# A written order for the expert stage's TensorE, VectorE and ScalarE work, with a split lead of 7 to 3 tiles, 7 of 14 down tiles kept in float32, and three more tile buffers

## The chip, the core and the metric

The kernel runs on one core of one Trainium2 chip. The core has five engines with a queue each: PE (TensorE, whose weight loads the profile shows as PEld), DVE (VectorE), ACT (ScalarE), POOL (GpSimd) and SP (SyncE, which here only issues DMAs). Each engine works its own queue strictly in the order of the program; semaphores tie them together. The metric is the device time in microseconds. The median of three runs of the kernel before is 1290.66 us (1288.96 to 1290.76).

## The reference

Two layers over 256 positions of width 1024. Each layer runs a mixer and a channel mixer. The second layer's channel mixer is the stage that this case is about: eight experts of width 3584, and each position takes its two best.

```python
def swiglu(x, wg, wu, wd):
    return (jax.nn.silu(x @ wg) * (x @ wu)) @ wd

def moe_swiglu(h, w_router, wg, wu, wd):
    xt = h.reshape(-1, d)
    logits = (xt @ w_router).astype(jnp.float32)
    top_v, top_i = lax.top_k(logits, TOP_K)
    gates = jax.nn.softmax(top_v, axis=-1)
    comb = jnp.sum(jax.nn.one_hot(top_i, N_EXPERTS) * gates[..., None], axis=1)
    y = jnp.zeros_like(xt)
    for e in range(N_EXPERTS):
        y = y + comb[:, e:e + 1] * swiglu(xt, wg[e], wu[e], wd[e])
    return y.reshape(bsz, s, d)
```

All weights are float32 in HBM.

## The kernel before

**Tiles.** All large weights come as one stream of 406 tiles of 128 x 2048 float32 (1 MB). Tiles 0 to 69 belong to the first mixer, the dense layer and the second mixer; tiles 70 to 405 are the experts': eight experts times 14 column groups (`NG`) times three tiles (gate, up, down). One group of one expert is called a step here, numbered n = 0 to 111. `MOE` is 70.

**Split.** A product is made of float16 parts. `split_tile` (L101) turns a raw tile into a high part on ACT (L114, called the heads) and a remainder on DVE (L115, the tails; it needs the heads). `mm3` (L276) then does three float16 products: high x high (L278), high x low (L279) and low x high (L280), which is the first to need the tails. Some down tiles are not split but used as they are in float32: `whole(i)` (L119) says so for groups 1, 4, 7 and 10 of the 14 (`WHOLE`), 32 tiles in all.

**A step.** `gate_up` (L414) does the 96 products of the gate and the up tile for the at most 80 positions of the expert (`CAP`); `hidden` (L436) makes silu on ACT (L446), the product on DVE (L450, or L448 where the down tile is whole) and, for a split down tile, its two float16 parts (L452 on ACT, L453 on DVE). `down` (L607) of the step before follows: 12 float16 products (L621) for a split tile, four float32 products (L615) for a whole one. Once per expert come `gather` (L548: 16 float32 products L558, parts L562 on ACT and L563 on DVE, for the next expert's input), `scatter_weights` (L593), `evacuate` (L625) and `combine` (L631: four float32 products L636, sums L637 on DVE).

**Buffers.** Raw tiles sit in `RAW` = 9 slots and, in the experts, in two more "spare" tiles put together from work buffers (`SPARE`, loaded as two halves each), again and again in a ring of 11. Split tiles sit in `SPLIT` = 9 buffers. A raw slot is free again when the tails are made, or, for a whole tile, when its `down` is done. `load` (L84) issues the DMAs on SP in tile order, and a DMA whose slot is still in use holds SP and every DMA behind it.

**Order.** The code calls `split` up to the step after the current one (L646), but the queue order of all engines is set by a scheduler at build time from its own estimates of durations; nothing in the code fixes where the heads of a tile stand against the silu of a step on ACT.

Of the kernel before, what the change touches and what calls it, by code (L numbers as in the profile page):

```python
# [7 lines left out]
F32 = mybir.dt.float32  # L8
F16 = mybir.dt.float16
# [22 lines left out]
RAW = 9  # L32
# [4 lines left out]
SPARE = (("gw", "ig"), ("a", "th"))  # L37

WHOLE = (1, 4, 7, 10)
# [13 lines left out]
def trunk(ctx: ExitStack, tc: tile.TileContext, x, w, small, gates, last, out):  # L53
# [27 lines left out]
    state = {"loaded": 0, "split": 0}  # L81
    NT = w.shape[0]

    def load(upto):  # L84
        while state["loaded"] < min(upto, NT):
# [14 lines left out]

    def split_tile(i, r):  # L101

        t = spl.tile([P, 2, 2048], F16, name="hl")
        fine = isinstance(i, int) and MOE + SPLIT - 1 <= i < MOE + SPLIT + 3
        with ExitStack() as order:
            if i == MOE + SPLIT - 1:
                for ins in behind:
                    order.enter_context(tc.issue_after(ins))
            for sl, src in r:
                n = sl.stop - sl.start  # L110
                step = 512 if fine else n
                for k in range(0, n, step):
                    to = slice(sl.start + k, sl.start + k + step)
                    S.activation(t[:, 0, to], src[:, k:k + step], AF.Copy, scale=SW)  # L114
                    V.scalar_tensor_tensor(t[:, 1, to], src[:, k:k + step], SW, t[:, 0, to], op0=OP.mult,  # L115
                                           op1=OP.subtract)
        parts[i] = [t[:, 0], t[:, 1]]

    def whole(i):  # L119

        return i >= MOE and (i - MOE) % 3 == 2 and (i - MOE) // 3 % NG in WHOLE

    def split(upto):
        while state["split"] < min(upto, NT):
# [7 lines left out]
            load(i + 1 + RAW + (len(SPARE) if i >= MOE else 0))  # L132
# [281 lines left out]
    def gate_up(ig, iu, h, n, between=None):  # L414

        if isinstance(iu, int):
            split(iu + 1)
# [77 lines left out]
    def moe(l, accs, extra_load):  # L495
        base = pos["t"]
        gcol = par["nf"][:, l * 8:(l + 1) * 8]
# [50 lines left out]
        def gather(e):  # L548
            oh = wk.tile([P, 2, CAP], F32, name="oh", tag="rs", bufs=2)
            for c in range(2):  # L550
                V.tensor_scalar(oh[:, c], iota1, slot[:, c, e:e + 1], rS[:, c:c + 1], op0=OP.is_equal, op1=OP.mult)
            he = wk.tile([P, KD, 2, CAP], F16, name="he", tag=("uc", "ge")[e % 2])
            for q in range(4):
# [283 lines left out]
```

## Time and profile before

| | us |
|---|---|
| median of three runs | 1290.66 |
| the profiled execution, its own time | 1290.75 |
| its span, first to last instruction | 1288.9 |
| PE busy | 1193.8 (93%) |
| DVE busy | 1056.8 (82%) |
| ACT busy | 868.0 (67%) |

The span is 1.85 us shorter than the execution's own time. "Busy" is time with an instruction on the engine; PE's matmuls are pipelined, so its share is no measure of how close it is to its peak. The experts take the stretch from about 416 us to the end.

### The profile page before, as it was taken

The numbers are of one execution on the slowest core, as the hardware profiler recorded it, in microseconds if no ns is written. First come the engines' busy times: TensorE is split into PE (matmuls) and PEld (weight loads), VectorE is DVE, ScalarE is ACT, GpSimd is POOL, SyncE is SP. The second block draws the span as 40 slices with busy tenths as digits, with TensorE's granted clock in tenths as the row PEclk, the third lists the DMA queues.
The fourth block names the chain that finished last, engine by engine and source line by source line (L and its number), as shares of the span: only waits on it lengthen the run. The fifth ranks groups of instructions, "written<-read, shape, count | busy, mean of one in ns | idle before, by whom it ended". The sixth has DMA issues, their size and how long they took to land. (4 is left out here: it accounts for less than half of the span.)

```text
span 1288.9 us, 35355 instructions
## 1 busy us (share of the span) xinstructions
PE 1193.8 (93%) x15792; PEld 934.6 (73%) x15792; DVE 1056.8 (82%) x1083; ACT 868.0 (67%) x942; POOL 0.8 (0%) x7
## 2 busy tenths in 40 slices
PE   7999999999999999999899888999898899989986
PEld 5888888888889777776566666666766666666663
DVE  7797655567886998988788989898798898989885
ACT  6965444445674977768567767776677687777774
POOL 0000000000000000000000000000000000000000
PEclk9999999999997999999899999999999999999997
DMA  9975555554554999999999999999999999999970
GB/s 366 372 280 220 204 198 199 205 207 172 199 191 160 363 414 417 407 417 408 394 399 382 416 364 382 419 351 417 417 416 395 416 419 414 418 418 399 417 317 35
DMA packets 69282, 431.87 MB, mean 335 GB/s; under 512 B 7808, under 2 KB 7936, under 8 KB 24960
## 3 DMA queue, kind: packets, MB, share of 16 engines
q1 hardware_dynamic: 69120, 429.52, 83.6%
q8 instruction: 125, 2.05, 0.6%
q14 instruction: 37, 0.30, 0.1%
HBM read 428.44 MB, written 1.05 MB: 333 GB/s over the span
## 5 line engine op out<-in xcount | busy, mean ns | idle before, releaser
L115 DVE SCALAR_TENSOR_TENSOR hl<-raw,hl 128x2048 f16<-128x2048 f32 (+2 forms) x336 | 728.3, 2190 | 141.9 <-ACT hl L114 140.2
L114 ACT ACTIVATE hl<-raw 128x2048 f16<-128x2048 f32 (+2 forms) x336 | 603.2, 1824 | 94.4 <-PE mm L280 87.0
L280 PEld LDWEIGHTS <-hl 128*128 128x128 f16 x4704 | 469.0, 100 | 117.2 <-DVE hl L115 90.7
L278 PEld LDWEIGHTS <-hl 128*128 128x128 f16 x4704 | 470.4, 100 | 53.8 <-issue 18.7
L279 PEld LDWEIGHTS <-hl 128*128 128x128 f16 x4704 | 470.6, 100 | 32.3 <-issue 11.3
L280 PE MATMUL mm<-he,hl 128*128 128x80 f16 x3584 | 410.2, 203 | 59.2 <-DVE hl L115 57.1
L278 PE MATMUL mm<-he,hl 128*128 128x80 f16 x3584 | 416.0, 203 | 7.4 <-ACT hl L114 6.9
L279 PE MATMUL mm<-he,hl 128*128 128x80 f16 x3584 | 415.7, 203 | 0.0
L621 PE MATMUL acc<-hl,hdm 128*80 128x512 f16 x960 | 233.5, 382 | 2.1 <-DVE hdm L453 1.2
L278 PE MATMUL mm<-h,hl 128*128 128x256 f16 x768 | 209.3, 274 | 3.0 <-ACT h L228 2.8
L279 PE MATMUL mm<-h,hl 128*128 128x256 f16 x768 | 209.8, 274 | 1.8 <-DVE h L229 1.6
L280 PE MATMUL mm<-h,hl 128*128 128x256 f16 x768 | 209.9, 274 | 0.8 <-DVE hl L115 0.8
L621 PEld LDWEIGHTS <-hdm 128*80 128x80 f16 x960 | 102.5, 118 | 73.3 <-issue 3.3
L446 ACT ACTIVATE sg<-mm 128x160 f32<-128x160 f32 x112 | 33.7, 301 | 149.5 <-PE mm L280 149.4
L615 PE MATMUL acc<-raw,hdm 128*80 128x512 f32 x216 | 101.5, 599 | 0.0
L279 PE MATMUL acc<-hd,hl 128*128 128x256 f16 x224 | 60.9, 273 | 0.2 <-DVE hd L453 0.2
L280 PE MATMUL acc<-hd,hl 128*128 128x256 f16 x224 | 60.9, 273 | 0.0
L278 PE MATMUL acc<-hd,hl 128*128 128x256 f16 x224 | 60.6, 273 | 0.0
L452 ACT ACTIVATE hdm<-sg 128x160 f16<-128x160 f32 x80 | 26.7, 333 | 48.2 <-DVE sg L450 48.0
L615 PEld LDWEIGHTS acc<-raw,hdm 128*80 128x80 f32 x216 | 29.1, 151 | 34.9 <-issue 34.6
L636 PE MATMUL mm<-ye,sgt 80*128 80x512 f32 x64 | 37.0, 715 | 4.3 <-ACTq L664 3.1
L558 PE MATMUL mm<-oh,xt 128*128 128x80 f32 x256 | 35.6, 295 | 0.5 <-DVE sg L450 0.5
(207 smaller groups left out, 854.0 us busy)
## 6 DMA issues: line engine op xcount, KB each, us to landing
raw<-in_w SPq DMA_DIRECT2D x345, 1024.0 KB, 12.2
gw<-in_w SPq DMA_DIRECT2D x29, 512.0 KB, 11.8
ig<-in_w SPq DMA_DIRECT2D x29, 512.0 KB, 12.1
a<-in_w SPq DMA_DIRECT2D x29, 512.0 KB, 11.5
th<-in_w SPq DMA_DIRECT2D x29, 512.0 KB, 12.0
raw<-in_w SPq DMA_DIRECT2D x6, 512.0 KB, 11.9
xT<-in_x SPq DMA_DIRECT2D x4, 256.0 KB, 3.7
gw<-in_gates SPq DMA_DIRECT2D x2, 512.0 KB, 9.9
```

The lines of the kernel that those rows point to most:

```text
L114: S.activation(t[:, 0, to], src[:, k:k + step], AF.Copy, scale=SW)
L115: V.scalar_tensor_tensor(t[:, 1, to], src[:, k:k + step], SW, t[:, 0, to], op0=OP.mult, op1=OP.subtract)
L278: PE.matmul(o, wt[0][:, cols], a_hi, start=start, stop=False, skip_group_check=True)
L279: PE.matmul(o, wt[0][:, cols], a_lo, start=False, stop=False, skip_group_check=True)
L280: PE.matmul(o, wt[1][:, cols], a_hi, start=False, stop=stop, skip_group_check=True)
L446: S.activation(sg, bank[:, 0], AF.Silu, scale=scale)
L452: S.activation(hd[:, 0, sl], hf, AF.Copy)
L558: PE.matmul(o[:, z], xt[:, c, k * P:(k + 1) * P], oh[:, c], start=(z == 0 and c == 0), stop=(c == 1), skip_group_check=True)
L615: PE.matmul(eaccs[e][q], hd[:, c], wt[c][:, q * half:(q + 1) * half], start=(g == 0 and c == 0), stop=(g == NG - 1 and c == 1), skip_group ...
L621: PE.matmul(eaccs[e][q], hd[:, part, c], wt[wpart][:, c * D + q * half:c * D + (q + 1) * half], start=(g == 0 and c == 0 and part == 0 and ...
L636: PE.matmul(o, sgt[e][:, c * P:(c + 1) * P], ye[:, sl], start=True, stop=True)
```

## The change

Before the experts the engines' order stays as it was. `RAW` goes from 9 to 11, and there are three spares, (gw, ig), (a, th) and (cs, r), each used once, for tiles 90, 91 and 92. The room for the two more slots comes from a smaller DMA scratch (`dynamic_dma_scratch_size=1024`). `whole` takes every sixth tile, the down tile of each odd step: 56 tiles, seven of 14 per expert. In the experts the queues of PE, DVE and ACT follow the program text (`tc.manual_schedule`), while SP's is still set by the scheduler. A step is written as: `gate_up`, half a `combine` or a quarter of a `gather` where one is due, the `down` of the step before; on ACT and DVE beside it the heads and tails of two or three tiles, with silu behind the first heads. Splits run `LEAD` tiles ahead of the step's up tile, 7 falling to 3 over the 112 steps (as whole numbers: 7 in the first step, then 6, 5, 4 and 3 for about a quarter each), and heads one tile further.

```diff
-RAW = 9
+RAW = 11
-SPARE = (("gw", "ig"), ("a", "th"))
-WHOLE = (1, 4, 7, 10)
+SPARE = (("gw", "ig"), ("a", "th"), ("cs", "r"))
+LEAD = (7.0, 3.0)
+FIRST_SPARE = MOE + 9 + RAW
     def load(upto):
-            at = (i - MOE - SPLIT - RAW) % (RAW + len(SPARE))
-            if i >= MOE + SPLIT + RAW and at < len(SPARE):
+            at = i - FIRST_SPARE
+            if 0 <= at < len(SPARE):
     def whole(i):
-        return i >= MOE and (i - MOE) % 3 == 2 and (i - MOE) // 3 % NG in WHOLE
+        return i >= MOE and (i - MOE) % 6 == 5
+        def next_heads():
+            ...
+            heads(*halves[i])
+        def next_tails():
+            ...
+            todo["n"] += 1
+            tails(*halves.pop(i))
+            load(i + 1 + RAW + len(SPARE))
+            for n, (e, g) in enumerate(steps):
+                bank = gate_up(ig, iu, lambda part, k: he[:, k, part], CAP)[0]
+                if ready is not None and n > 1:
+                    combine(*ready, c=(g - 1))
+                ...
+                if 8 <= g < 12 and e + 1 < NE:
+                    gather_products(e + 1, g - 8)
+                if n:
+                    down(*before)
+                used = 2 * (n + 1) + (n + 1) // 2
+                lead = LEAD[0] + (LEAD[1] - LEAD[0]) * n / (len(steps) - 1)
+                k = max(0, used + int(lead) - todo["n"])
+                ...
+                if n == 0:
+                    next_heads()
+                for j in range(k + 2):
+                    if j < k:
+                        next_heads()
+                    if j == 0:
+                        S.activation(sg, bank[:, 0], AF.Silu, scale=IN_SCALE)
+                    if j < k:
+                        next_tails()
+                    if j == 0:
+                        V.scalar_tensor_tensor(hd if whole(idn) else hf, bank[:, 1], ...)
+                    if j == 1 and not whole(idn):
+                        S.activation(hd[:, 0], hf, AF.Copy)
+                        V.tensor_tensor(hd[:, 1], hf, hd[:, 0], op=OP.subtract)
+                ...
+        with tc.manual_schedule(engines={mybir.EngineType.PE, mybir.EngineType.DVE, mybir.EngineType.Activation}):
+            before = groups()
```

ACT's queue at steps 46 to 48 (the fourth expert), before: sg is the silu of a step, hl the heads of a tile, hdm the high part of the step's result.

```order
L446 ACTIVATE sg_10982<-mm 128x160
L114 ACTIVATE hl<-raw 128x2048 x4
L446 ACTIVATE sg_11111<-mm 128x160
L114 ACTIVATE hl<-raw 128x2048
L452 ACTIVATE hdm<-sg_11112 128x160
L114 ACTIVATE hl<-raw 128x2048 x2
L446 ACTIVATE sg_11234<-mm 128x160
L114 ACTIVATE hl<-raw 128x2048
L452 ACTIVATE hdm<-sg_11235 128x160
L114 ACTIVATE hl<-gw 128x1024
L114 ACTIVATE hl<-ig 128x1024
```

The same steps on ACT in the changed kernel (sgt is a copy that falls into step 46 once per expert):

```order
L737 ACTIVATE sg_10790<-mm 128x160
L113 ACTIVATE hl<-raw 128x2048
L745 ACTIVATE hdm<-sg_10791 128x160
L754 ACTIVATE sgt<-mm 80x256
L113 ACTIVATE hl<-raw 128x2048
L737 ACTIVATE sg_10920<-mm 128x160
L113 ACTIVATE hl<-raw 128x2048 x3
L737 ACTIVATE sg_11041<-mm 128x160
L113 ACTIVATE hl<-raw 128x2048
L745 ACTIVATE hdm<-sg_11042 128x160
L113 ACTIVATE hl<-raw 128x2048
```

The kinds of work stay the same; what moves is which tiles' heads these are (further ahead of the step), and the regular two or three per step.

PE's queue around the gather of the second expert's input, in the first expert's step 11, before:

```order
L280 MATMUL mm<-he,hl 128x80
L558 MATMUL mm<-oh,xt 128x80 x16
L615 MATMUL acc<-raw,hdm 80x512 x4
L278 LDWEIGHTS hl
L278 MATMUL mm<-he,hl 128x80
```

In the changed kernel, the second of four such places (step 9 of the first expert):

```order
L289 MATMUL mm<-he,hl 128x80
L574 MATMUL mm<-oh,xt 128x80 x4
L639 MATMUL acc<-raw,hdm 80x512 x4
L287 LDWEIGHTS hl
L287 MATMUL mm<-he,hl 128x80
```

The 16 products in one block have become four products in each of the steps 8 to 11, between `gate_up` and `down`.

SP's queue from the last load ahead of the experts on, before (cs<-in_last is a constant for the end of the kernel; TENSOR_LOAD reads the longest list):

```order
L94 DMA raw<-in_w 128x2048
L727 DMA cs<-in_last 128x1024
L94 DMA raw<-in_w 128x2048 x5
L650 TENSOR_LOAD mxi
L650 ISA x2
L94 DMA raw<-in_w 128x2048 x6
L94 DMA gw<-in_w 128x1024
L94 DMA ig<-in_w 128x1024
L94 DMA a<-in_w 128x1024
L94 DMA th<-in_w 128x1024
L94 DMA raw<-in_w 128x2048 x9
```

In the changed kernel:

```order
L97 DMA raw<-in_w 128x2048
L97 DMA cs<-in_w 128x1024
L97 DMA raw<-in_w 128x2048 x2
L760 TENSOR_LOAD mxi
L760 ISA x2
L97 DMA raw<-in_w 128x2048 x10
L834 DMA cs<-in_last 128x1024
L97 DMA raw<-in_w 128x2048 x301
L97 DMA raw<-in_w 128x1024 x4
```

The spares no longer return; the constant now stands behind twelve expert loads, where it waits until tile 92, which sits in cs, is split.

## Rows read from the trace of the kernel before

**Rows 1.** The page: span, and busy time of each engine.

```profile
span 1288.9 us, 35355 instructions
PE 1193.8 (93%) x15792; PEld 934.6 (73%) x15792; DVE 1056.8 (82%) x1083; ACT 868.0 (67%) x942; POOL 0.8 (0%) x7
```

**Rows 2.** Stretches: from:to, length, busy by engine, granted clock, DMA share, GB/s.

```profile
480.00:1200.00 720.00, 657.76 (x10195) 481.28 (x10192) 626.17 (x558) 517.50 (x527) 0.00 (x0) 0.99 1.00 404
1200.00:1250.00 50.00, 46.26 (x711) 32.87 (x708) 42.74 (x33) 37.82 (x33) 0.00 (x0) 0.97 0.99 406
1250.00:1252.00 2.00, 2.00 (x39) 1.40 (x38) 2.00 (x2) 0.00 (x0) 0.00 (x0) 1.00 0.13 53
1000.00:1150.00 150.00, 137.31 (x2151) 100.78 (x2152) 131.12 (x117) 109.91 (x115) 0.00 (x0) 1.00 1.02 416
500.00:550.00 50.00, 50.00 (x785) 36.60 (x784) 44.29 (x41) 36.29 (x38) 0.00 (x0) 1.00 1.01 410
800.00:850.00 50.00, 45.15 (x676) 33.46 (x674) 42.96 (x44) 35.69 (x42) 0.00 (x0) 0.97 1.02 419
```

**Rows 3.** Waits from 416 to 1271 us: who waited for whom, us, times, longest.

```profile
PEld L280 <- DVE hl L115: 89.5, 96, 2.7
PEld L278 <- ACT hl L114: 11.7, 16, 3.2
ACT sg L446 <- PE mm L280: 149.4, 91, 6.9
DVE hl L115 <- ACT hl L114: 68.3, 61, 3.3
DVE hl L115 <- DMA th<-in_w: 1.5, 1, 1.5
SPq L94 <- PE acc L615: 109.7, 27, 11.3
```

**Rows 4.** Timeline of ACT: the silus of steps that PE runs without a wait.

```profile
540.14 0.30 ACT L446 ACTIVATE sg<-mm 128x160 f32<-128x160 f32 x1 [1.04 <-PE mm L280]
...
546.12 0.30 ACT L446 ACTIVATE sg<-mm 128x160 f32<-128x160 f32 x1 [1.12 <-PE mm L280]
...
553.09 0.30 ACT L446 ACTIVATE sg<-mm 128x160 f32<-128x160 f32 x1 [1.80 <-PE mm L280]
```

**Rows 5.** Groups by form, 460 to 1240 us: count, busy us, mean ns, idle before.

```profile
L115 DVE SCALAR_TENSOR_TENSOR hl<-raw,hl 128x2048 f16<-128x2048 f32 x221 | 499.0, 2284 | 64.8 <-ACT hl L114 63.3 <-DMA th<-in_w 1.5
L114 ACT ACTIVATE hl<-raw 128x2048 f16<-128x2048 f32 x219 | 408.9, 1900 | 0.8 <-PE mm L280 0.8
L115 DVE SCALAR_TENSOR_TENSOR hl<-ig,hl 128x1024 f16<-128x1024 f32 x27 | 32.8, 1214 | 0.0
L446 ACT ACTIVATE sg<-mm 128x160 f32<-128x160 f32 x101 | 30.5, 302 | 142.6 <-PE mm L280 142.4
L453 DVE TENSOR_TENSOR hdm<-sg,hdm 128x160 f16<-128x160 f32 x72 | 22.8, 317 | 3.0 <-ACT hdm L452 3.0
L637 DVE TENSOR_TENSOR xT<-mm,xT 128x512 f32<-128x512 f32 x24 | 15.8, 684 | 5.6 <-PE mm L636 5.4
L563 DVE SCALAR_TENSOR_TENSOR he<-mm,sm,he 128x80 f16<-128x80 f32 x56 | 14.7, 293 | 9.4 <-ACT he L562 9.4
```

**Rows 6.** Timeline of PE near 700 us: gather, whole down, split down.

```profile
701.70 2.09 PEld L558 LDWEIGHTS mm<-oh,xt 128*128 128x128 f32 x18
...
703.78 3.60 PE L615 MATMUL acc<-raw,hdm 128*80 128x512 f32 x8
...
708.06 1.46 PE L621 MATMUL acc<-hl,hdm 128*80 128x512 f16 x6
```

**Rows 7.** The entry: SP's issues from 397 to 446 us.

```profile
397.55 0.33 SPq L727 DMA_DIRECT2D cs<-in_last  x1
416.57 29.61 SPq L94 DMA_DIRECT2D raw<-in_w  x11
```

**Rows 8.** Timeline: ACT's first silu, PE's last down; then the chain's combine.

```profile
419.57 1.28 ACT L446 ACT_TABLE_LOAD   x1
420.87 0.30 ACT L446 ACTIVATE sg<-mm 128x160 f32<-128x160 f32 x1
...
1268.22 2.32 PE L621 MATMUL acc<-hl,hdm 128*80 128x512 f16 x10
...
1273.64 7.21 PE mm L636 x8
```

**Rows 9.** Stretches of 5 us with a low DMA rate or a low clock.

```profile
765.00:770.00 5.00, 5.00 (x73) 3.22 (x72) 5.00 (x3) 4.31 (x3) 0.00 (x0) 1.00 0.69 257
855.00:860.00 5.00, 5.00 (x72) 3.22 (x68) 4.98 (x4) 2.26 (x3) 0.00 (x0) 1.00 0.43 152
830.00:835.00 5.00, 5.00 (x67) 3.72 (x65) 5.00 (x4) 3.01 (x4) 0.00 (x0) 0.70 1.03 420
```

More of the change, by code (lines that the diff above doesn't have):

```diff
@@ L496, in moe @@
         base = pos["t"]
+        state["experts"] = True
+        split(MOE + 8)
+        load(FIRST_SPARE + len(SPARE))
         gcol = par["nf"][:, l * 8:(l + 1) * 8]
@@ L567, in moe, with gather_products @@
-        hes = {0: gather(0)}
-        gathered = hes[0][1]
+                V.tensor_scalar(lists[e][:, c], iota1, slot[:, c, e:e + 1], rS[:, c:c + 1], op0=OP.is_equal,
+                                op1=OP.mult)
+            hes[e] = wk.tile([P, KD, 2, CAP], F16, name="he", tag=("uc", "ge")[e % 2])
+        def gather_products(e, q):
+            o = got[e, q] = mm((P, 2, CAP))
+            for z in range(2):
+                k = 2 * q + z
+                for c in range(2):
+                    PE.matmul(o[:, z], xt[:, c, k * P:(k + 1) * P], lists[e][:, c], start=(z == 0 and c == 0),
+                              stop=(c == 1), skip_group_check=True)
@@ L637, in combine @@
                     V.tensor_tensor(yt[:, c, sl], o, (xt if e == 0 else yt)[:, c, sl], op=OP.add)
-        before, ready = None, None
-        for e, g in steps:
-            ig, iu, idn = take(3)
-            he = hes[e][0]
-            banks = gate_up(ig, iu, lambda part, k: he[:, k, part], CAP)
-            hd = [P, 2, CAP] if whole(idn) else [P, 2, 2, CAP]
-            hd = hidden(banks, CAP, wk.tile(hd, F32 if whole(idn) else F16, name="hdm", tag="xs", bufs=2))
-            split(idn + 1 + 3)
-            if g == 3:
-                scatter_weights(e)
-            if e == 0 and g == 2:
-                longest = nc.values_load(mxi[0:1, 0:1], min_val=0, max_val=T)
-            if e == NE - 1 and g == 0:
-                extra_load()
-            if g == 11 and e + 1 < NE:
-                hes[e + 1] = gather(e + 1)
-            if ready is not None:
-                combine(*ready)
-                ready = None
-            if before is not None:
-                down(*before)
-                if before[1] == NG - 1:
-                    ready = (before[0], evacuate(before[0]))
-            before = (e, g, idn, hd)
+        for i in (MOE + 8, MOE + 9):
+            t = spl.tile([P, 2, 2048], F16, name="hl")
+            with ExitStack() as order:
+                if i == MOE + 8:
+                    for ins in behind:
+                        order.enter_context(tc.issue_after(ins))
+                for hi, lo, src in split_pieces(raw.pop(i), t, 512):
+                    S.activation(hi, src, AF.Copy, scale=SW)
+                    V.scalar_tensor_tensor(lo, src, SW, hi, op0=OP.mult, op1=OP.subtract)
+            parts[i] = [t[:, 0], t[:, 1]]
@@ new lines, in moe @@
+        todo = {"heads": MOE + 10, "tails": MOE + 10, "n": 9}
+        halves = {}
+        def next_heads():
+            while todo["heads"] < NT and whole(todo["heads"]):
+                i = todo["heads"]
+                parts[i] = [t[:, k:k + D] for _, t in raw.pop(i) for k in range(0, t.shape[1], D)]
+                todo["heads"] += 1
+            i = todo["heads"]
+            if i == NT:
+                return
+            todo["heads"] += 1
+            t = spl.tile([P, 2, 2048], F16, name="hl")
+            halves[i] = (raw.pop(i), t)
+            heads(*halves[i])
+            parts[i] = [t[:, 0], t[:, 1]]
```

130 lines of the change are left out of this document (86 added, 44 removed).

## The prediction

> **What bounds the kernel now.** I read the page first: PE is busy for 93% of the span and DVE for 82% [rows 1], which says that several engines are near their limit and not which of them ends last. So I went to the experts' stage, from 416 us on, and read three things there. The stretches: from 480 to 1200 us the DMA moves 404 GB/s, but over 1000 to 1150 us it holds 416 [rows 2]. So DMA runs at 97% of a rate that it can hold, and 3% is lost in places; two of them are in [rows 9] (257 and 152 GB/s over 5 us). The waits: PE waits 89.5 us in 96 pieces for the tails of a split and 11.7 us for heads [rows 3], 101 us in all, 0.9 us a step. ACT waits 149.4 us for `gate_up` at the silu, and DVE 68.3 us for heads, but only one wait, of 1.5 us, is for a landing [rows 3]. So the tiles are there and the splits come late. The reader should see a loop in this: the silu stands in ACT's queue and waits for PE; heads behind it, of tiles that have long landed, wait too; DVE's tails wait for the heads; and PE, one step on, waits for the tails. The timeline of ACT shows the same steps without that wait: 5.98 us from silu to silu with a split down and 6.97 us with a whole one [rows 4].
>
> So two limits stand close together: the loop sets the pace, and the DMA is 3% behind it. The last load lands at about 1251 us, when 53 GB/s are left over 2 us [rows 2]; the last `down` ends at 1268.22 + 2.32 = 1270.5 us [rows 8], and 18.4 us of combine, norm and output follow to the end of the span [rows 1, 8]. All the tiles that were landed or split by 1251 us still had to go through PE.
>
> **The change, part by part.**
>
> *Written order, lead 7 to 3.* It takes the heads that PE needs next out from behind the silu that PE must release: a tile is split three to six tiles ahead of the step that uses it. What PE must do with no wait, per expert: seven steps of 5.98 and seven of 6.97 us [rows 4] are 90.7 us; the gather has 32 pieces at 2.09 / 18 = 0.116 us, 3.7 us [rows 6]; the combine took 7.21 us at the end at half the clock, so 3.6 us at full clock [rows 8]. That is 98.0 us, or 7.0 us a step. DVE, per expert: 35 tails x 2.28 = 79.8; 21 small ones x 0.32 = 6.7; eight of 0.29 and four of 0.68 are 5.1; with lists some 93 us [rows 5]. ACT: 35 x 1.90 = 66.5, and with its small ones some 77 us [rows 5]. DMA: 42 tiles of 1.049 MB at 416 GB/s are 105.9 us [rows 2]. The order of limits is then DMA, PE, DVE, ACT, if no wait is left. In a pair of steps DVE has 5 tails and 3 small ones, 12.4 us, against 12.95 us of PE, so the tails hold a lead where it exists. With the lead at 3, the up tile of the next step is only just ready: silu 0.30, two tails and two small ones, 5.5 us, against a whole down of 3.44 us and half of a `gate_up` (1.7 us), so about 0.4 us lost in every second step of the last quarter, 6 us in all. PE has 0.56 us a step to spare against DMA, which covers it.
>
> *Seven whole down tiles instead of four.* It removes 24 splits (24 x 2.28 = 55 us of DVE, 24 x 1.90 = 46 us of ACT) and adds 24 x 0.99 = 24 us to PE [rows 4, 5]. In a DMA-bound stage none of the three is on the path. Without that cover PE pays the 24 us.
>
> *Buffers.* Before, SP stands idle from 397.55 to 416.57 us for want of a slot [rows 7]. Now three more tiles are loaded in this gap (3.1 MB, 7.6 us at 416 GB/s). Against it: the spares free no slot of the ring when they are split, and the constant for the end holds SP until tile 92 is split, so part of the gain can be given back before 480 us. I bound it by 0 and 7.6 us and take 5.
>
> *Reading the longest list* moves from the end into step 2 on three engines. The rows do not show it in such a place; I take it as nothing, within 1 us either way, since all three engines have slack there.
>
> *DMA's end.* From 480 us on the kernel before moved 720 x 404 + 50 x 406 + 2 x 53 GB/s, that is 311.3 MB [rows 2]. At a steady 416 GB/s this takes 748 us and ends at 1228; less 5 us for the spares, 1223 us.
>
> The Trainium skill's page "DMA: Bandwidth & Descriptors" (Specifications) gives a limit of some 358 GB/s from HBM for one core; at that rate the same bytes would end at about 1341 us and the run at about 1371. The trace does not agree: 416 GB/s held for 150 us [rows 2], and the measurement decides.
>
> *From the last landing to the last down.* The last tile is a whole one, the last split tile (up) lands 2.5 us ahead of it. Its two half heads are made while DVE is busy with the gate tile's tails and a product, until about 0.5 us before the last landing; DVE then makes the two half tails of 1.21 us [rows 5] by 1.9 us after it; half a `gate_up` 1.7, a split down 2.6 (12 x 1.46 / 6 = 2.9, less the pipeline's end) and a whole down 3.44 (3.60, less the same) [rows 6] follow: 9.6 us after the landing. Then come the same 18.4 us.
>
> *Sum:* 1223 + 9.6 + 18.4 = 1251 us of span. The profiled execution's own time lies 1.85 us above its span (1290.75 against 1288.9) and 0.09 above the median, so 1253 us for the run: 3% faster. Its own bounds: 419 GB/s and all three tiles give 480 + 308.2 / 0.419 = 1216 and a run of 1246, less some 3 us if the tail is better packed; 410 GB/s [rows 2] and no tile give 1239 and a run of 1269. So 1243 to 1269.
>
> **The rivals.**
>
> *PE still waits, in part.* PE without a wait would run from 416 us (its first silu is at 420.87 and was late by a table load [rows 8]) for 8 x 90.7 + 7 x 3.7 + 7 x 3.6 = 776 us to 1192, and DMA allows 1232.6, so 40 us of waits, 0.36 a step, are free. If half of the 102 us stay, the last down is at 1243 and the run at 1263; at 70% it is 1284. For it: nothing measured says that the engines hold their lead through a combine, where DVE's queue now waits for two products of PE ahead of its tails. Against it: 0.45 us a step to regain.
>
> *The loop stays and the float32 price comes on top (slower).* This is one mechanism: ACT's fixed queue stands at heads or at a silu whose release is behind another engine's work, and PE waits as long as before. All 101 us of waits and 24 us more of float32 give 1291 + 24 = 1314. It is slower from the point where more than 77% of the waits stay. For it: each silu still has one tile's heads ahead of it, which can stand for a landing. Against it: the silu's result is needed only after the next `gate_up`, whose weights are split already.
>
> *Whole tiles hold the ring (slower).* A whole tile keeps its slot until its `down`. Before, 32 of them cost SP 109.7 us of waiting in 27 pieces [rows 3], and with that most of the 24 us of DMA that were lost (772 us for what 416 GB/s does in 748). With 56 whole tiles, 1.75 times that is 42 us: DMA ends at 1265, the run at 1295, 0.3% slower. It decides where DMA loses more than 38 us in all. Against it: the loads now wait for slots in the order in which the written queues free them, and the ring reaches some nine tiles past the heads. The Trainium skill's page "Perfetto Trace Analysis" (Optimization Strategy) reads a gap that repeats on the engine that should be saturated as a possible want of buffers; by that rule the dips of [rows 9] would come back more often here, and the trace agrees so far as SP's waits for whole tiles go.
>
> *It does not do what it says:* the written queues end up with the same waits for other reasons and the same pace, 1291.
>
> **How the numbers follow.** Forecast 0.66 (1243 to 1269, likeliest 1253); PE waiting in part 0.16 (1263 to 1285); the loop staying 0.06; the ring 0.05; no effect 0.04; still better than the forecast's range 0.03. What a measurement of this kernel can tell from no change is 0.2%, 2.6 us. Faster by more: 0.66 + 0.16 + 0.03 = 0.85. Same: 0.04. Slower: 0.11. The range 1242 to 1281 takes in the forecast and most of the first rival and leaves 0.18 to 0.2 out.
>
> **What would show it.** Right: DMA at 414 GB/s or more in nearly all stretches from 480 us to its end near 1223; PE's waits for tails under 40 us; ACT and DVE now waiting for landings in the later experts; about 28 us from the last landing to the end of the span; steps near 7.5 us in the later experts. The ring rival would show in SP's waits for whole downs and in dips of the DMA; the loop in ACT's waits at the silu next to PE's waits for tails. A granted clock that falls in PE's new gaps, as to 0.70 at 830 us [rows 9], would make it wrong, and so would a DMA that holds less than 410 GB/s when it never pauses.

## The result and the profile after

The changed kernel takes 1255.32 us (median of four runs, 1253.93 to 1257.14), the kernel before 1290.07 us beside it: a ratio of 0.9732, 95% interval 0.9715 to 0.9749, so 2.7% less. The forecast was 1253 us, 1242 to 1281. The profiled execution of the changed kernel has its span at 1253.5 us and its own time at 1255.41.

The page of the changed kernel, the lines that answer to [rows 1]:

```profile
span 1253.5 us, 34604 instructions
PE 1199.8 (96%) x15696; PEld 931.6 (74%) x15696; DVE 997.5 (80%) x978; ACT 821.2 (66%) x837; POOL 0.8 (0%) x7
```

Its stretches, with the columns of [rows 2]:

```profile
416.00:460.00 44.00, 43.54 (x729) 32.93 (x727) 38.35 (x44) 36.95 (x41) 0.00 (x0) 0.97 0.84 324
460.00:480.00 20.00, 20.00 (x334) 15.68 (x333) 17.86 (x17) 13.72 (x14) 0.00 (x0) 1.00 1.00 407
480.00:1200.00 720.00, 693.23 (x10612) 499.56 (x10610) 608.66 (x494) 504.00 (x459) 0.00 (x0) 0.99 1.01 419
...
1040.00:1045.00 5.00, 4.14 (x74) 3.17 (x73) 5.00 (x4) 4.17 (x3) 0.00 (x0) 1.00 0.93 369
...
1215.00:1220.00 5.00, 3.95 (x56) 2.89 (x57) 2.41 (x3) 4.01 (x4) 0.00 (x0) 1.00 0.62 251
1220.00:1225.00 5.00, 4.58 (x102) 3.88 (x100) 5.00 (x4) 4.07 (x5) 0.00 (x0) 1.00 0.49 202
...
1227.00:1228.00 1.00, 1.00 (x3) 0.25 (x2) 1.00 (x3) 0.40 (x2) 0.00 (x0) 1.00 0.08 33
```

From 480 to 1200 us the loads now run at 419 GB/s, where the kernel before had 404 [rows 2], and the share of the DMA engines is at or above 1 nearly all the way. The last load lands at 1228.0 us, not at 1251.6. The reader should also see what was not foreseen: from 416 to 480 us the loads are slower than before (324 and 407 GB/s in the two stretches where it was 353 and 418), and in the last 14 us they fall to half (share 0.49). Both are taken up below. The two stretches of the kernel before:

```profile
416.00:460.00 44.00, 42.11 (x733) 32.14 (x731) 43.01 (x50) 38.47 (x44) 0.00 (x0) 0.99 0.92 353
460.00:480.00 20.00, 19.79 (x343) 14.81 (x340) 20.00 (x18) 16.49 (x17) 0.00 (x0) 1.00 1.01 418
```

Waits of the changed kernel from 416 to 1240 us (who waited for whom: us, times, longest), which answer to [rows 3]:

```profile
ACT hl L113 <- DMA raw<-in_w: 171.0, 158, 3.6
...
ACT sg L737 <- PE mm L289: 40.5, 31, 3.8
...
PEld L289 <- DVE hl L117: 9.1, 18, 0.7
...
SPq L97 <- DVE hl L117: 254.6, 110, 7.0
SPq L97 <- DMA raw<-in_w: 227.3, 123, 2.8
...
SPq L97 <- PE acc L639: 47.7, 24, 5.5
```

The picture is turned round. PE's waits for tails fell from 89.5 to 9.1 us and ACT's at the silu from 149.4 to 40.5 ([rows 3] reach to 1271 us; to 1240 it was 85.8 and 142.4); in their place ACT waits 171 us, 158 times, for landings. An engine that waits for data which has not come is the sign that the loads set the pace.

The end of PE's work in the timeline (start, length: the last split down, the last whole one, then the combine), which answers to [rows 8]:

```profile
1231.44 2.76 PE L645 MATMUL acc<-hl,hdm 128*80 128x512 f16 x12
1234.03 3.60 PE L639 MATMUL acc<-raw,hdm 128*80 128x512 f32 x8
1239.52 5.51 PE L660 MATMUL mm<-ye,sgt 80*128 80x512 f32 x8 [1.89 <-ACTq L771]
```

The 35.4 us by which the span is shorter have two parts: the last landing comes 23.6 us earlier (1251.6 to 1228.0), and what follows it takes 25.5 us instead of 37.3. The last `down` ends at 1237.6, 9.6 us after the last landing, where it had been 18.9 us (1270.5): PE no longer has a backlog of landed tiles.

### The profile page after: what moved, and what is told of

The parts are those of the page before. It is cut to its first block, busy times and chain, and to the rows that moved or that the text cites. A ratio compares the mean times of both kernels' runs of the same rounds, so it can differ in the third digit from the quotient of the medians.

```text
span 1253.5 us, 34604 instructions
## 1 busy us (share of the span) xinstructions
PE 1199.8 (96%) x15696; PEld 931.6 (74%) x15696; DVE 997.5 (80%) x978; ACT 821.2 (66%) x837; POOL 0.8 (0%) x7
## 3 DMA queue, kind: packets, MB, share of 16 engines
q8 instruction: 124, 2.03, 0.7%
## 5 line engine op out<-in xcount | busy, mean ns | idle before, releaser
L113 ACT ACTIVATE hl<-raw 128x2048 f16<-128x2048 f32 x269 | 509.2, 1901 | 172.3 <-DMA raw<-in_w 171.0
L117 DVE SCALAR_TENSOR_TENSOR hl<-raw,hl 128x2048 f16<-128x2048 f32 x269 | 607.5, 2275 | 18.3 <-ACT hl L113 17.8
L289 PE MATMUL mm<-he,hl 128*128 128x80 f16 x3584 | 398.9, 202 | 6.7 <-DVE hl L117 6.6
L287 PE MATMUL mm<-he,hl 128*128 128x80 f16 x3584 | 399.0, 202 | 0.0
L288 PE MATMUL mm<-he,hl 128*128 128x80 f16 x3584 | 399.0, 202 | 0.0
L125 DVE SCALAR_TENSOR_TENSOR hl<-raw,hl 128x2048 f16<-128x2048 f32 (+1 forms) x78 | 176.0, 2261 | 72.0 <-ACT hl L124 71.8
L124 ACT ACTIVATE hl<-raw 128x2048 f16<-128x2048 f32 (+1 forms) x78 | 146.1, 1880 | 93.4 <-PE mm L289 86.2
L639 PE MATMUL acc<-raw,hdm 128*80 128x512 f32 x448 | 202.4, 594 | 0.0
L645 PE MATMUL acc<-hl,hdm 128*80 128x512 f16 x672 | 159.3, 388 | 13.1 <-ACT hdm L745 13.0
L639 PEld LDWEIGHTS acc<-raw,hdm 128*80 128x80 f32 x448 | 64.0, 151 | 97.6 <-issue 97.4
L645 PEld LDWEIGHTS <-hdm 128*80 128x80 f16 x672 | 76.6, 119 | 77.4 <-ACT hdm L745 14.8
L737 ACT ACTIVATE sg<-mm 128x160 f32<-128x160 f32 x112 | 32.8, 293 | 40.6 <-PE mm L289 40.5
L741 DVE SCALAR_TENSOR_TENSOR sg<-mm,sg 128x160 f32<-128x160 f32 x56 | 18.0, 321 | 36.3 <-ACT sg L737 36.2
```

Of the source, the lines that this page charges most:

```text
L113: S.activation(hi, src, AF.Copy, scale=SW)
L117: V.scalar_tensor_tensor(lo, src, SW, hi, op0=OP.mult, op1=OP.subtract)
L124: S.activation(hi, src, AF.Copy, scale=SW)
L125: V.scalar_tensor_tensor(lo, src, SW, hi, op0=OP.mult, op1=OP.subtract)
L287: PE.matmul(o, wt[0][:, cols], a_hi, start=start, stop=False, skip_group_check=True)
L288: PE.matmul(o, wt[0][:, cols], a_lo, start=False, stop=False, skip_group_check=True)
```

## The experiments

The theory: with the splits in a written order the loads are the bound of the experts, and PE, DVE and ACT work in their shadow. The rivals: PE (or a loop between the engines) still sets the pace; or it is not the order that helped, but the smaller amount of split work, or the buffers. Eight kernels in one table ("GB/s" from 480 to 1200 us, "landing" by the landing records of each trace, "rest" from there to the end of the span). The kernels ran in five sets, in which the kernel before had medians of 1290.1, 1290.4, 1291.3, 1292.4 and 1292.3 us, so a difference between kernels of different sets is good to about 2 us:

| kernel | order | float32 downs | slots, spares | us | GB/s | landing | rest |
|---|---|---|---|---|---|---|---|
| before | scheduler | 4 of 14 | 9 + 2 returning | 1290.1 | 404 | 1251.6 | 37.3 |
| before_7of14 | scheduler | 7 | 9 + 2 returning | 1275.7 | 410 | 1244.4 | 28.1 |
| before_raw11 | scheduler | 4 | 11 + 2 returning | 1279.0 | 409 | 1237.7 | 37.0 |
| before_both | scheduler | 7 | 11 + 2 returning | 1266.1 | 412 | 1234.5 | 29.3 |
| order_alone | written | 4 | 9 + 2 returning | 1268.1 | 415 | 1240.0 | 26.1 |
| order_4of14 | written | 4 | 11 + 3 once | 1255.7 | 419 | 1229.0 | 26.3 |
| ring9 | written | 7 | 9 + 3 once | 1259.2 | 417 | 1234.7 | 23.2 |
| after | written | 7 | 11 + 3 once | 1255.3 | 419 | 1228.0 | 25.5 |

The remaining ones (lead3, last_on_act, act_lead8, less_dma, low8, less_instr) change one thing in the changed kernel each and are told one by one.

### Is it the loads that set the pace?

The bytes of the loads are cut, and nothing else: the second half of some 103 down tiles is left out, and the first half is read twice in its place.

```diff
+            half_only = i >= FIRST_SPARE + len(SPARE) and (i - MOE) % 3 == 2 and i < NT - 2
             for sl, t in raw[i]:
+                if half_only:
+                    t, sl = t[:, 0:D], slice(0, D)
                 nc.sync.dma_start(t, w[i][:, sl])
+            if half_only:
+                raw[i] = [(slice(0, 2 * D), t[:, None, :].to_broadcast([P, 2, D]))]
...
```

> The changed kernel, but from tile 93 on only the first half of each down tile is loaded, and both halves of the split or of the float32 products read that half; the number and the shapes of the products and of the splits stay, so what is left out is half of the bytes of some 103 down tiles, 54 MB or 129 us of loading at 419 GB/s. Theory (the pace of the loads): with 0.5 MB less in each step the loads need 88 us per expert, less than PE's 98, so PE becomes the bound: last down near 416 + 776 + 10 to 20 of waits, run at 1222 to 1232, and ACT no longer waits for landings (171 us before this edit). Rival (PE, or a loop between the engines, already sets the pace, and the loads only fill what is left): the time stays at 1250 to 1255.

Measured: 1216.01 us, 39 us less. Its stretch and its waits (416 to 1240 us; lines shifted by the edit, L298 is the low x high product, L126 the tails, L750 the silu):

```profile
480.00:1200.00 720.00, 716.91 (x11103) 519.70 (x11101) 628.26 (x513) 516.27 (x479) 0.00 (x0) 1.00 0.93 359
```

```profile
ACT sg L750 <- PE mm L298: 137.3, 96, 5.1
...
PEld L298 <- DVE hl L126: 2.9, 6, 0.7
```

PE is now busy for 716.91 of 720 us and waits 2.9 us for tails; ACT's waits are at the silu again, for PE, and none for landings is among its long ones. So the written order lets PE run without a break, and some 1216 us is what PE alone allows. The changed kernel's 1255 is set by the loads. My expectation of 1222 to 1232 was missed by 6 us: it granted PE 10 to 20 us of waits that it doesn't have.

### What are the three more float32 downs worth?

```diff
     def whole(i):
-        return i >= MOE and (i - MOE) % 6 == 5
+        return i >= MOE and (i - MOE) % 3 == 2 and (i - MOE) // 3 % NG in (1, 4, 7, 10)
-                used = 2 * (n + 1) + (n + 1) // 2
+                used = 2 * (n + 1) + sum(not whole(MOE + 3 * m + 2) for m in range(n))
```

> The changed kernel with the old choice of float32 down tiles (groups 1, 4, 7 and 10, four of 14); the written order, the lead and the buffers stay. It asks what the three more float32 tiles of each expert are worth. Theory (the experts now go at the pace of the loads): per expert DVE rises from some 93 to 100 us and ACT from 77 to 83, both still under the 105 us that 42 tiles take at 419 GB/s, and PE falls by 3 us that nobody waits for, so the time stays at 1255 us, within 4. Rival 1 (the splits still set the pace, the float32 tiles are what helped): 3 x 2.28 us of tails more per expert, up to 55 us in all, 1275 to 1310. Rival 2 (PE sets the pace): 24 x 0.99 = 24 us less of PE, 1231.

Measured: 1255.67 us, the same as the changed kernel, as the theory had it, with 24 more tiles to split. Its stretch shows DVE at 656 of 720 us where it was 609, the loads at the same 419 GB/s, and its ACT still waits for landings, only less:

```profile
480.00:1200.00 720.00, 684.17 (x10696) 508.69 (x10694) 656.46 (x536) 546.61 (x502) 0.00 (x0) 0.98 1.01 419
```

```profile
ACT hl L113 <- DMA raw<-in_w: 98.2, 125, 3.5
...
PEld L289 <- DVE hl L117: 20.5, 33, 1.9
```

Under the written order with the larger ring the float32 downs are worth nothing, and their 24 us on PE cost nothing. Without the order it is otherwise:

```diff
-WHOLE = (1, 4, 7, 10)
+WHOLE = (1, 3, 5, 7, 9, 11, 13)
```

> The kernel before with seven of 14 down tiles in float32 (groups 1, 3, 5 ... 13) and nothing else: the scheduler's order, nine slots and two spares in the ring. Theory (the loop of silu, heads, tails and products set the pace, by the order of the queues, not by the amount of split work): PE's waits stay near 100 us and 24 us of float32 products come on top in part, 1295 to 1314. Rival (the amount of split work was the limit): 55 us of tails and 46 us of heads less take PE's waits away, and the loads then bound it, 1262 to 1272.

Measured: 1275.74 us, a ratio of 0.989 (0.9874 to 0.9907). Neither case was right. The same edit that does nothing in the changed kernel takes 14.6 us off the one before. By the table the last landing comes 7.2 us earlier and the rest is 9.2 us shorter: less split work means less backlog behind the last landing.

### What are the slots worth, and do the three parts add up?

```diff
-RAW = 9
+RAW = 11
-    nc = bacc.Bacc("TRN2", target_bir_lowering=False, num_devices=1)
+    nc = bacc.Bacc("TRN2", target_bir_lowering=False, num_devices=1, dynamic_dma_scratch_size=1024)
```

> The kernel before with 11 slots instead of nine (and the smaller DMA scratch that makes room), its two spares in the ring as they were, nothing else. It asks what buffers do alone. Theory (the order of the queues set the pace, the tiles had landed anyway): two more tiles in the gap ahead of the experts, but PE waits for tails as before, 1284 to 1291. Rival (SP's 109.7 us of waits for whole downs held the loads back): the dips of the loads go, 1262 to 1275.

Measured: 1278.98 us, 0.992 (0.9899 to 0.9941): 11.4 us less, between the two ranges. The smaller DMA scratch was not tried without the slots. Waits of the kernel before, of this one, then of before_7of14, from 416 to 1240 us:

```profile
PEld L280 <- DVE hl L115: 85.8, 92, 2.7
...
SPq L94 <- DMA raw<-in_w: 81.1, 53, 2.5
```

```profile
PEld L280 <- DVE hl L115: 77.3, 84, 2.6
...
SPq L94 <- DMA raw<-in_w: 373.9, 192, 3.3
SPq L94 <- PE acc L615: 90.3, 21, 17.7
```

```profile
PEld L280 <- DVE hl L115: 62.5, 78, 2.2
...
SPq L94 <- DMA raw<-in_w: 256.1, 136, 4.6
SPq L94 <- PE acc L615: 159.4, 39, 15.1
```

Here my reading of [rows 3] fell. In before_raw11 PE waits for tails nearly as long as before (77.3 us against 85.8 in this window), and yet the kernel is 11.4 us faster. What changed is on SP: it waits 373.9 us for an earlier load to land, that is, because loads are underway, where before it waited for slots and only 81.1 us for loads. So PE's waits were not the price that I took them for. The time of the kernel before was the loads' end plus a backlog, and the loads stood still at times for want of a free slot. In the table this kernel's last landing is 13.9 us earlier and its rest the same: slots bring the loads forward and leave the backlog.

Both edits together, without the written order:

> The kernel before with both other parts of the change and without the written order: seven of 14 down tiles in float32, and 11 slots with the two spares in the ring. Alone they took off 14.6 us (float32) and 11.4 us (slots). Theory (the queues' order still keeps splits behind silus, so SP still finds no slot at times): the two gains at most add up, 1262 to 1268, with the loads at 411 to 415 GB/s from 480 to 1200 us and 50 us or more of PE's waits for tails. Rival 1 (enough slots and less split work are all that the loads needed, the written order adds nothing): 1254 to 1258 with 418 GB/s or more. Rival 2 (both mend the same loss): 1272 to 1276.

Measured: 1266.05 us, 25.2 us under the kernel before in the same set. The gains of 14.6 and 11.4 us add up to within 1 us, the loads run at 412 GB/s, and PE still waits 55.5 us for tails: the theory. And the order alone, with the float32 downs and the ring of the kernel before:

```diff
-RAW = 11
+RAW = 9
-SPARE = (("gw", "ig"), ("a", "th"), ("cs", "r"))
+SPARE = (("gw", "ig"), ("a", "th"))
-            at = i - FIRST_SPARE
+            at = (i - FIRST_SPARE) % (RAW + len(SPARE)) if i >= FIRST_SPARE else -1
-        return i >= MOE and (i - MOE) % 6 == 5
+        return i >= MOE and (i - MOE) % 3 == 2 and (i - MOE) // 3 % NG in (1, 4, 7, 10)
-                used = 2 * (n + 1) + (n + 1) // 2
+                used = 2 * (n + 1) + sum(not whole(MOE + 3 * m + 2) for m in range(n))
-    nc = bacc.Bacc("TRN2", target_bir_lowering=False, num_devices=1, dynamic_dma_scratch_size=1024)
+    nc = bacc.Bacc("TRN2", target_bir_lowering=False, num_devices=1)
```

> The written order and its lead alone: four of 14 down tiles in float32 as before, nine slots and two spares that return in the ring of 11 as before. Theory (the order alone takes the splits out of the loop and frees slots as fast as tiles land): 1255 to 1264, the loads at 415 GB/s or more from 480 to 1200 us, PE's waits for tails under 40 us. Rival (without the two slots the loads still find the ring full behind whole downs and late splits): 1270 to 1282, the loads at 405 to 411.

Measured: 1268.09 us, between the two ranges: 4 us over the theory's and 2 us under the rival's. The theory's signs came (the loads at 415 GB/s, PE's waits for tails at 21.1 us), its time did not. The order alone takes off 23 us and shortens the rest from 37.3 to 26.1 us, but the loads run at 415, not 419 GB/s, so the rival has a part in it. The step from here to order_4of14, slots and spares with the smaller scratch, is some 12 us (1268.1 to 1255.7). The ring with seven float32 downs and fewer slots:

```diff
-RAW = 11
+RAW = 9
```

> The changed kernel with nine slots instead of 11; the three spares, used once, stay, and so do the order and the seven float32 downs. In the steady part the ring holds nine tiles, two fewer than the kernel before had with its returning spares. Theory (a slot is held from the issue of its load over some 19 us of transfer to the end of its split or its down, so nine slots leave only six or seven loads outstanding at 419 GB/s, which is enough): 1256 to 1262, a shift of two tiles at the entry (5 us) and little after it. Rival (whole tiles hold the ring): the loads pause at whole downs, 405 to 412 GB/s, 1270 to 1285.

Measured: 1259.21 us, 3 to 4 us over the changed kernel, in the theory's range. The intervals of the two ratios overlap (0.9738 to 0.9770 against 0.9715 to 0.9749), so how much of it is real is open. Stretch and SP's waits for whole downs (416 to 1240 us):

```profile
480.00:1200.00 720.00, 689.11 (x10540) 497.26 (x10539) 603.86 (x491) 501.36 (x457) 0.00 (x0) 0.99 1.01 417
```

```profile
SPq L97 <- DVE hl L117: 474.5, 203, 8.6
SPq L97 <- PE acc L639: 116.5, 42, 6.1
```

SP waits 116.5 us for whole downs, more than in the kernel before, and the loads still hold 417 GB/s: nine slots are full nearly all the time, which is what a queue of outstanding loads looks like from SP. A long wait of SP for a slot is no loss as long as the DMA share stays at 1.

### What is the lead worth?

```diff
-LEAD = (7.0, 3.0)
+LEAD = (3.0, 3.0)
```

> The changed kernel with a lead of three tiles from the first step on, not seven falling to three; nothing else. Theory (with the loads as the bound a tile can be split only when it has landed, and PE's loss of some 0.4 us in every second step fits into the 0.4 us a step that PE has to spare): 1255 to 1260; up to 5 us later if the raw slots are freed later in the first expert, where tiles are there in advance. Rival (the lead is what broke the loop, at three the waits for tails come back): PE waits 40 to 80 us for tails, 1265 to 1290.

Measured: 1261.27 us, some 5 us more (ratio to before 0.9768, 0.9747 to 0.9789, where the changed kernel has 0.9732), which the theory allowed for in the first expert. Its stretches:

```profile
416.00:460.00 44.00, 43.31 (x731) 32.71 (x730) 31.88 (x41) 31.80 (x37) 0.00 (x0) 0.98 0.75 286
460.00:480.00 20.00, 20.00 (x331) 15.58 (x328) 18.00 (x17) 13.72 (x14) 0.00 (x0) 1.00 0.96 376
480.00:1200.00 720.00, 688.72 (x10543) 496.50 (x10541) 608.41 (x494) 505.00 (x460) 0.00 (x0) 1.00 1.01 418
```

The loss is read at the entry: 38 GB/s less over 44 us and 31 less over 20 us are 2.3 MB, 5.5 us at 419 GB/s. From 480 us on a lead of three is as good as one of seven, although PE's waits for tails go from 9.1 to 28.3 us, still under the rival's 40.

### The entry

Two tries to get back what is lost from 416 to 480 us. The constant for the end is issued from ACT's queue, which stands in the last expert there:

```diff
-        nc.sync.dma_start(late["gl"], last.partition_broadcast(P))
+        nc.scalar.dma_start(late["gl"], last.partition_broadcast(P))
```

> The changed kernel, with the load of the constant for the end (cs<-in_last) issued from ACT's queue, where it stands in the last expert's first step, instead of SP's, where it stands behind twelve expert loads and holds SP from 447.5 to 455.8 us until tile 92 is split. Theory (that wait takes back a part of what the three preloaded tiles gave): the loads no longer fall to 269 to 365 GB/s from 450 to 465 us, 3 us of loading are kept to the end, 1251 to 1253. Rival (no slot was free then anyhow, the ring paces the entry): 1254 to 1257.

Measured: 1254.20 us, ratio to before 0.9706 (0.9685 to 0.9727), in the rival's range. From 450 to 465 us its loads move 314 GB/s where the changed kernel has 331, so the sign of the theory did not come. The same with a lead that starts at eight, `LEAD = (8.0, 3.0)`:

> The changed kernel with the constant for the end issued from ACT's queue and the lead starting at eight tiles instead of seven (eight in the first step only, then falling to three), so that one more tile is split in the first step, where the loads fall to 151 GB/s at 425 to 430 us for want of a free slot. Theory (the entry is short of slots because no tails are written into step 0): up to 3 us of loading come back at 420 to 435 us beside the 1 to 3 us of the constant's move, 1249 to 1252. Rival (the nine split buffers are all taken there, so the added split only waits for PE and holds the silu behind it): 1254 to 1257.

Measured: 1254.56 us, 0.9719 (0.9705 to 0.9732). From 425 to 430 us it has 259 GB/s where the changed kernel has 151, and loses it again by 460 (319 against 324 over 416 to 460 us). Neither interval is clear of the changed kernel's 0.9715 to 0.9749, so neither edit is shown to help. From 416 to 480 us SP of the changed kernel waits 31.0 us for tails, that is, for slots that a split frees; that an earlier free slot would shorten the run is argued and not shown.

### The halved loads at the end

In the trace each load's landing is recorded in 16 parts, which are read here as one for each of the 16 DMA engines. In the changed kernel the parts drift apart: at 500 us the eighth part lands 2 us before the last, at 700 us 4.5, at 900 us 8, at 1200 us 12. So eight of the core's 16 DMA engines run ahead of the other eight by some five loads, and at the end they have nothing left for some 12 us while the others finish; the share of 0.49 agrees. In the kernel before, where the loads paused often, the distance at the end is 2.6 us.

To see whether it is a standing difference of two halves, two late loads were put on eight engines alone:

```diff
+LATE = (401, 402)
...
-                nc.sync.dma_start(t, w[i][:, sl])
+                src = w[i][:, sl]
+                if i in LATE:
+                    src = late_w[LATE.index(i)].rearrange("(b a) c -> a b c", a=8)
+                nc.sync.dma_start(t, src)
...
```

> The changed kernel, with the loads of tiles 401 and 402 read from a copy whose rows lie in another order, so that the access pattern's slowest dimension is eight and, by the Trainium skill's page DMA: Bandwidth & Descriptors (its section on why a DMA increments its semaphore by 16), the transfer runs on the lowest-numbered eight of the core's 16 DMA engines alone; bytes and results stay. In the changed kernel's trace the DMA share falls to a half (0.49) at 1220 to 1225 us, when the loads still outstanding are equal shares on all engines: so half of the engines have finished some 12 us ahead of the others. Theory A (half of the engines lag all along, and it is the higher-numbered half): two tiles put on the leading half take 5 us off the lagging one, the last load lands near 1223 and the run takes 1250 to 1251. Theory B (the lagging half is the lower-numbered one): the last load lands 5 us later, 1259 to 1261. Rival (the halved share at the end is something else, such as the smaller pieces of the last two tiles): within 2 us of 1255.

Measured: 1274.61 us. Its stretches:

```profile
1195.00:1200.00 5.00, 5.00 (x56) 2.71 (x54) 4.57 (x4) 2.95 (x3) 0.00 (x0) 1.00 1.02 423
1205.00:1210.00 5.00, 4.57 (x97) 3.82 (x96) 3.76 (x4) 2.88 (x3) 0.00 (x0) 1.00 0.99 213
1220.00:1225.00 5.00, 3.23 (x49) 3.04 (x48) 2.52 (x2) 0.02 (x1) 0.00 (x0) 0.50 0.96 202
```

The distance goes from 10.0 to 20.4 us, 5.2 us for each of the two loads, which is a 1 MB load at 200 GB/s. So it was the lagging half that got them (theory B), and the direction was right; the size was not. From 1205 to 1225 us only 202 to 213 GB/s move. The ordinary loads ahead of the two now land 5 us apart instead of 2.5, so the two are not queued behind them but share the lagging engines with them; SP waits 18.5 us for earlier loads to land between 1200 and 1235 and issues little that is new, and the last load lands some 22 us later than in the changed kernel, not 5. That the leading half stands idle meanwhile is read from the rate; the share near 1 would then be two packets underway at a time on each of the other eight, which is argued and not shown. The rule behind the edit, that of the Trainium skill's page "DMA: Bandwidth & Descriptors" (🔬 Why a DMA increments its semaphore by 16 and not by 1), says that such a transfer runs on the lowest-numbered eight engines. The halved rate agrees with eight engines; no run here shows which numbers they have.

What makes one half lag? Besides the loads only one kind of traffic is steady: that of the page's "instruction" queues, the larger of which has 124 packets and 2.03 MB in the changed kernel. A kernel with far fewer instructions and the same loads:

```diff
-                    mm3(o[a][c], wts[a], slice(k * 256 + c * P, k * 256 + (c + 1) * P), h(0, k), h(1, k),
-                        start=(k == 0 and (a, c) in first), stop=(k == KD - 1))
+                    cols = slice(k * 256 + c * P, k * 256 + (c + 1) * P)
+                    if n == CAP:
+                        PE.matmul(o[a][c], wts[a][1][:, cols], h(0, k), start=(k == 0 and (a, c) in first),
+                                  stop=(k == KD - 1), skip_group_check=True)
+                        continue
+                    mm3(o[a][c], wts[a], cols, h(0, k), h(1, k), start=(k == 0 and (a, c) in first), stop=(k == KD - 1))
```

> The changed kernel with a third of the products of the experts' gate and up tiles: only high x tail is left, the two products with the tile's heads are left out, so the result is not the reference's; loads, splits, downs and all order stay. It takes some 12 of the 38 us that PE needs per expert for gate_up's other two thirds off PE (64 of 96 products and as many weight loads in each step) and with them some 45% of all instructions of the program. Theory A (the loads are the bound, PE's work is hidden under them): the loads' end and the run move by less than 5 us; after the last landing some 1 us less is left to do. Theory B on the lag between the two halves of the DMA engines (the loading of instructions goes over the lagging half only and makes its lag): the stretch of half share at the end shrinks from some 12 to 5 to 8 us, the last landing comes 2 to 3 us earlier, the run takes 1250 to 1252. Rival to B: the stretch stays at 12 us. Rival to A (PE sets the pace of the steps): the run falls by 20 us or more.

Measured: 1243.70 us, 12 to 13 us less than the changed kernel, so both theories had the time wrong (theory A less than 5 us of change, theory B 1250 to 1252), and the rival to A (20 us or more) did too. That DMA queue in the changed kernel and in this one (packets, MB, share of 16 engines), then two stretches of this one:

```profile
q8 instruction: 124, 2.03, 0.7%
```

```profile
q8 instruction: 68, 1.11, 0.4%
```

```profile
480.00:1200.00 720.00, 545.97 (x4387) 301.65 (x4386) 611.52 (x495) 508.06 (x462) 0.00 (x0) 0.88 1.01 421
1200.00:1220.00 20.00, 14.71 (x115) 7.20 (x113) 17.09 (x13) 13.04 (x13) 0.00 (x0) 0.91 0.68 280
```

With 41% fewer instructions (20267 for 34604) the distance of the halves at the end is 4.1 us instead of 12, the loads run at 421 GB/s and the last lands at 1218.4 us, 9.6 us earlier. The expectation counted only the lag, (12.1 - 4.1) / 2 = 4.0 us of this; 2 GB/s over 720 us are 3.4 more, and 332 and 420 GB/s instead of 324 and 407 from 416 to 480 us some 1.5. The rest, 22.5 us instead of 25.5, makes up the difference of the spans. PE's busy time falls by 147 us in the 720, and the run by 12 to 13: that PE does not set the pace is seen once more. The lag falls with the instruction traffic, but this edit also takes work off PE, and so does not part the two by itself.

The landing records of the changed kernel do. From one load to the next the 16 parts keep their distances, but for single steps in which one part lands over 0.9 us later than its pace. From 700 to 1195 us, where the halves stand apart, there are 57 such steps (median 1.55 us) against 56 packets of that instruction queue; 53 of the packets have a step within the 5 us after their start, and 53 of the steps are in the lagging eight parts. ring9, with the same PE work and nine slots, shows the same (57 steps, 54 of them in the lagging eight; 54 of 56 packets with a step). So nearly every one of these packets holds back one engine, and it is nearly always one of the lagging half: that is what makes it lag; which numbers these engines have the trace does not name. That PE's lighter use also helps the loads a little is not excluded.

## Why the prediction was right, and where it was not

- **The bound (right in the end, wrong for the kernel before).** "The loop sets the pace, and the DMA is 3% behind it" named the two things, but took PE's 101 us of waits for the first limit. before_raw11 keeps those waits and is 11.4 us faster. What held the time was a backlog behind the last landing and loads that paused for want of slots; the loop was one of three ways in which slots came free late, the amount of split work and the size of the ring the others. Each of the three edits alone takes 11 to 23 us, but the float32 downs, worth 14.6 us alone, are worth 0.4 under the written order and the larger ring.
- **Written order (right).** PE without a wait: less_dma ends its last `down` at 1199 us, the working said 1192. PE's waits for tails are 9.1 us, foretold under 40. Silu to silu is 7.2 to 7.4 us within each of the last five experts, foretold near 7.5. ACT waits for landings as foretold (171 us); DVE does not, it waits behind ACT (17.8 us for heads).
- **Seven float32 downs off the path (right).** order_4of14 against the changed kernel: 0.4 us, inside both ranges. "Without that cover PE pays the 24 us" was wrong for the kernel before: before_7of14 gains 14.6 us, since 101 us of engine time for splits went.
- **Buffers (mis-sized).** The working counted only the entry, 5 us. The entry gave less: of the three preloaded tiles one was left at 480 us (110 loads in where it had been 109; from 416 to 480 us the loads moved 44 x 324 + 20 x 407 GB/s, 22.4 MB, where it had been 23.9), 2.5 us. But in the steady part the slots count: 415 to 419 GB/s and some 12 us from order_alone to order_4of14, 3 to 4 us from ring9.
- **DMA's end (1223 foretold, 1228 measured).** Three errors, and not all one way: 419 GB/s instead of 416 takes off some 5 us; one tile kept instead of two adds some 2.5; and the halves of the DMA engines add 7.6. From 480 us 310.2 MB at 419 GB/s would have ended at 1220.4; the halved rate from about 1214 us on costs the other 7.6 us. The term of the halves was not in the working at all, nor in [rows 2], where the fall to 53 GB/s takes 2 us.
- **From the last landing to the last down (right):** 9.6 us foretold, 9.6 measured. What follows took 15.9 us, not 18.4: the combine took 5.51 us where it had taken 7.21, at a mean granted clock of 0.69 (1239 to 1245 us) where it was 0.52 (1273 to 1281 us), and PE waited 1.89 us ahead of it instead of 3.09.
- **Lead (right where it was spoken of).** The smaller lead costs nothing late; at the entry, which the working did not treat, seven instead of three is worth some 5 us.
- **Rivals.** PE waiting in part and the loop with the float32 price: refuted by less_dma and by the 9.1 us of PE's waits for tails. Whole tiles holding the ring: SP's waits for whole downs fell from 109.7 to 47.7 us; in before_7of14 they rose to 159.4 and the time fell all the same, so the price that I read from [rows 3] was none. By the gap rule of the Trainium skill's page "Perfetto Trace Analysis" (Optimization Strategy) the dips would have come back more often; of the stretches of 5 us between 480 and 1200 us the changed kernel has only the three from 1040 to 1055 us below 400 GB/s (369, 378, 378). That more buffers help where the loads pause, as the rule has it, agrees with before_raw11.
- **The sum.** 5 us too little at the loads' end and 2.5 us too much at the tail left 2.3 us of error in the time: the mechanism held, but that the time came out so close is in part luck, since errors of up to 7.6 us cancelled. One side sum was wrong: at 358 GB/s the 311.3 MB would have ended at 1350 us; the 1341 us are for 308.2 MB. Nothing in the forecast rests on it.
- **Left open.** Reading the longest list in step 2 was not tried by itself. The smaller DMA scratch was not tried by itself. Which DMA engines lag was not told.

## What to carry to other kernels

Where two limits stand within a few per cent of each other, a wait on the engine with the highest busy share does not name the bound; look at whether the stream of loads ever pauses, and at what frees its buffers. Three edits that all free buffers earlier do not add up to their single gains once the loads run without a break, and from then on a cheaper split or a longer lead buys nothing. A ring that is always full is then a good sign, not a loss; what still counts is how early the stream begins, and what else uses the DMA engines, the loading of instructions among it.

## What the runs showed of the hardware

- One core held 419 to 421 GB/s of loads for 720 us. The limit of some 358 GB/s on the Trainium skill's page "DMA: Bandwidth & Descriptors" (Specifications) does not hold for this run. The Trainium skill's page "Perfetto Trace Analysis" (Engine Utilization) states for a single active core a ceiling of some 435 GB/s set by the 16 DMA engines; 421 fits under it.
- Two halves of the DMA engines drift apart under a load stream that never pauses, by some 1.5 us in 100 us, and the distance is paid at the end, 12 us at half rate. With 0.92 MB less of instruction traffic (and 147 us less of PE's work) the distance was a third and the last load 9.6 us earlier.
- A packet of the instruction queue (16 KB) held back one of the lagging eight DMA engines by some 1.55 us: 53 of 56 packets from 700 to 1195 us in the changed kernel.
- A load that runs on eight engines cost far more than its bytes at the end of a deep queue: 22 us for two loads of 1 MB, with 202 to 213 GB/s for the 20 us from 1205 us on.
